# S5 powers and chunk angles between the first projections, small copies on VectorE, and a head's split in two steps

## The chip, the cores and the metric

One core of one Trainium2 chip runs the whole kernel: TensorE (PE), VectorE (DVE), ScalarE (ACT) and GpSimd (POOL) beside SyncE (SP), which only issues transfers. The metric is device microseconds of one execution of the kernel, the median of several runs.

## What is computed

A backbone of two layers over 1024 latent tokens and 256 context tokens of 1024 channels. The even layer, in which the change lies, projects the normed tokens and runs two recurrences over the sequence in both directions: a real one (RG-LRU, 8 heads of 128 channels, behind a centred convolution of 4 taps) and a complex diagonal one (S5, 32 groups of 16 channels and 64 states). The odd layer is latent attention, and is not touched.

```python
def even_mix(h_ctx, h_lat, ...):
    xa_l, ga_l, ub_l, gb_l = jnp.split(h_lat @ w_in, EVEN_SPLITS, axis=-1)   # the same for ctx
    ya_c, ya_l = rglru_mix(xa_c, xa_l, conv_w, conv_b, wr, br, wi, bi, lam, with_ctx)
    yb_c, yb_l = s5_mix(ub_c, ub_l, lam_re, lam_im, log_dt, b_re, b_im, c_re, c_im, d_skip, glu_w, glu_b, with_ctx)
    return concat([ya * silu(ga), yb * silu(gb)]) @ w_out

def rglru_coeffs(u, wr, br, wi, bi, lam):          # u: convolved input of the head
    r = sigmoid(u @ wr + br); i = sigmoid(u @ wi + bi)
    log_a = -LRU_C * r * softplus(-lam)
    return exp(log_a), sqrt(-expm1(2 * log_a)) * (i * u)   # then h[t] = a h[t-1] + b

def s5_discretise(lam_re, lam_im, log_dt, b_re, b_im):
    dt = exp(log_dt); mag = exp(lam_re * dt)
    ab_re = mag * cos(lam_im * dt); ab_im = mag * sin(lam_im * dt)
    f = (ab - 1) / lam                             # complex
    return ab, f * b                               # then h[t] = ab h[t-1] + (f b) u[t]
```

## The kernel before, in words

All of it is one program for one core, written out in the order in which each engine gets its instructions; no scheduler reorders them. Matrix products take fp32 operands as a high part (`hi`, a cast on ScalarE) and a low part (`lo`, the difference, on VectorE) and add three products (`mm3`, L209 to L211). Tokens stand as 128 channels by 1280 columns (NT: 256 context, 1024 latent).

`start` (from L531, its last part is touched) norms the tokens and runs the first projections in pairs of 128 output channels, kept in PSUM banks `mm` and `g`. `pair` is a generator: each `next(run)` issues a part of a pair's products on PE, and between two of them the code puts work for the other engines. In order around the change: the pair with weights `w2` (heads 0 and 1 of the RG-LRU input); `convolve(h, banks)` for each of the two heads, that is `conv_in` (two ScalarE passes out of each bank into `xa` and `u`), three `conv_tap` on VectorE and `conv_parts`, which makes `hi` and `lo` of `u`; the pair with weights `w3` (S5 inputs); `lru_prep` (26 tiny VectorE operations on `lrusp`); `s5_small`, which makes 19 powers of each S5 eigenvalue (`Pre`, `Pim`), calls `s5_phases` and then makes the input factors `bb`. At step 7 of that last pair the first weights of the recurrence stage are split (`wh` L751, `wl` L752), and the S5 inputs leave PSUM as `chunks` (L603).

`s5_phases` (L431) makes, for 16 batches of two groups, the angle of every chunk of 8 tokens: four pieces, each of three VectorE operations (L438 to L440), four ScalarE activations (L441 to L444) and three transfers of 640 KB into the DRAM buffer `phdr`, issued by POOL (L446). The tiles of `big` (line 150) are 11 buffers of 5 KB a partition that are shared round-robin; a tile waits until the one that had its buffer before is done with, transfers included. `setup` is a pool of its own, opened in the space of an earlier pool once that is released.

`recurrences` runs 8 turns, one for each head. The order of each turn is written out by hand in `TURNS` (L64): the first row for turns 0 and 1, the second for turns 2 to 6, the third for turn 7. A word is a step, its arguments, and by how many turns its head or batch is older than the turn (`-`: one ahead). Capitals are steps of a head: `C` a tap, `I` the split `hi`, `lo`, `G` gate products, `A H Q` exponent, tanh and root on ScalarE, `M B D N` products and scan on VectorE. Small letters are steps of an S5 batch (three in each of turns 2 to 6, one in turn 7; L63): `l` loads, `k` decay, `a` products on PE, `s` rotation into `G` (L966 to L969), `r` the two scans over chunks into `H` (L977 to L982), `d` rotation back (L987 to L990), `o` products on PE and ScalarE's copy `y` (L1000). `P` are projection products and `W` weights that fill PE between.

Two of these steps end in a small copy on ScalarE: `s` extends G by its first 32 columns, `r` moves 32 columns of H behind two POOL memsets:

```python
tt(S, S, x.t2, ALU.add)
nc.scalar.copy(x.G[:, :, :, NCH:EXT], x.G[:, :, :, 0:32])     # L969, end of s
...
nc.gpsimd.memset(Hv[64:128, :, :, EXT - 1:EXT], 0.0)
nc.scalar.copy(Hv[64:128, :, :, 0:32], Hv[64:128, :, :, NCH:EXT])   # L982, end of r
```

Of the kernel before, what the change touches and what calls it, by code (L numbers as in the profile page):

```python
# [19 lines left out]
CH, NCH = 8, 160  # L20
# [12 lines left out]
def shape_constants():  # L33
# [18 lines left out]
    for a in (row, col):  # L52
# [80 lines left out]
class Kernel:  # L133
# [225 lines left out]
    def s5_small(self):  # L359
        nc, t, c, sp = self.nc, self.t, self.const, self.sp  # L360
        tt, ts, stt = nc.vector.tensor_tensor, nc.vector.tensor_scalar, nc.vector.scalar_tensor_tensor
        LR, LI, LD = self.s5p[:, 0], self.s5p[:, 1], self.s5p[:, 2]
        sm = sp.tile([128, 12, 32], F32, name="s5small")
        dt, lr, th, n_, u, den, nr, fr, fi, x1, x2 = (sm[:, i] for i in range(11))
        self.s5_rho = c.tile([128, 32], F32, name="s5rho")
        self.s5_u8 = c.tile([128, 32], F32, name="s5u8")
        nc.scalar.activation(dt, LD, AF.Exp)
        tt(lr, LR, dt, ALU.mult)
# [7 lines left out]
        NP = 19  # L376
        v = sp.tile([128, 32, NP], F32, name="s5v", tag="vx", bufs=4)
        w = sp.tile([128, 32, NP], F32, name="s5w", tag="vx", bufs=4)
        bc = lambda a, k: a.unsqueeze(2).to_broadcast([128, 32, k])
        kpow = sp.tile([128, 2, NP], F32, name="s5k")  # L380
        nc.sync.dma_start(kpow, t["kpow"])
        kk = lambda i: kpow[:, i].unsqueeze(1).to_broadcast([128, 32, NP])
        tt(v, bc(u, NP), kk(0), ALU.mult)
        ts(w, v, MAGIC, -MAGIC, ALU.add, ALU.add)
        tt(v, v, w, ALU.subtract)
# [7 lines left out]
        tt(w, bc(lr, NP), kk(1), ALU.mult)
        nc.scalar.activation(w, w, AF.Exp)
        nc.vector.tensor_copy(self.s5_rho, w[:, :, 18])
        Pre, Pim = hs, sn
        tt(Pre, hs, w, ALU.mult)
        tt(Pim, sn, w, ALU.mult)
        self.s5_phases()
# [31 lines left out]
    def s5_phases(self):  # L431
# [3 lines left out]
        for q in range(4):  # L435
# [4 lines left out]
            nc.vector.tensor_sub(v, v, n)  # L440
            nc.scalar.activation(n, v, AF.Abs)  # L441
# [89 lines left out]
    def start(self, outs):  # L531
# [91 lines left out]
        with self.tc.manual_schedule():  # L623
# [10 lines left out]
            self.load_const("s5p", "tau", "lru", "dmask", "s5d")  # L634
# [76 lines left out]
            for i in range(8):  # L711
# [144 lines left out]
    def recurrences(self, steps):  # L856
# [8 lines left out]
        class Head:  # L865
# [59 lines left out]
            def I(x):  # L925
                self.conv_parts(x.h)

        class Batch:
# [31 lines left out]
            def s(x):  # L960
# [8 lines left out]
                nc.scalar.copy(x.G[:, :, :, NCH:EXT], x.G[:, :, :, 0:32])  # L969

            def r(x):
# [10 lines left out]
                nc.scalar.copy(Hv[64:128, :, :, 0:32], Hv[64:128, :, :, NCH:EXT])  # L982
# [135 lines left out]
        def run(w, n):  # L1118
# [7 lines left out]
            elif (2 if k in "CI" else 0) <= n - age < 8:  # L1126
# [665 lines left out]
```

## Time and profile before

| what | value |
|---|---|
| median of 3 runs | 1636.22 us (1633.61 to 1636.89) |
| the profiled execution, its own time | 1638.18 us |
| its span (first to last instruction) | 1636.3 us |
| PE busy | 1504.2 us (92%) |
| VectorE, ScalarE, POOL busy | 1140.8, 835.5, 39.2 us |
| mean granted TensorE clock | 0.962 of full |

The profile is of one execution. The page gives busy time of each engine and the groups of costliest instructions; the trace behind it gives each instruction with its start, its duration and, in brackets, how long the engine idled before it and which instruction or transfer ended that (`<-`). The busy time includes nothing of register and semaphore instructions. Names on the left of `<-` in an instruction are what it writes, on the right what it reads; L is the line of the kernel.

### The profile page before, as it was taken

How to read it: one execution, taken by the hardware profiler on the slowest of the kernel's cores; microseconds unless marked ns; L12 is line 12 of the kernel's file. 1: busy time of each engine (PE TensorE's matmuls, PEld its weight loads, DVE VectorE, ACT ScalarE, POOL GpSimd, SP SyncE). 2: the span in 40 equal slices, each digit the busy share in tenths (PEclk: the TensorE clock that was granted, in tenths of full speed). 3: DMA queues.
4: the chain of work that ended last, by engine and by line, in shares of the span. 5: the costliest groups of instructions: out<-in, count | busy, mean ns of one | idle time of the engine just before them, and what ended most of it. 6: DMA issues, size and time to landing. Idle time of an engine off the chain costs nothing.

```text
span 1636.3 us, 22534 instructions
## 1 busy us (share of the span) xinstructions
PE 1504.2 (92%) x8690; PEld 1293.7 (79%) x8690; DVE 1140.8 (70%) x1827; ACT 835.5 (51%) x1441; POOL 39.2 (2%) x98
## 2 busy tenths in 40 slices
PE   7893797988888988799999999999999999999997
PEld 4672686776777777687787899978999999999887
DVE  6865479888988978832226443557888888889755
ACT  6544566586668567311115321545556555556532
POOL 0001100000000000000000000010000000000000
PEclk9897799999999999799999999999999999999999
DMA  9342542543435345555543132244011020122253
GB/s 352 104 143 97 199 140 88 175 125 117 133 106 163 118 136 200 214 206 180 190 150 139 52 104 78 81 163 134 17 46 55 30 70 19 56 91 84 78 179 124
DMA packets 94698, 201.93 MB, mean 123 GB/s; under 512 B 9728, under 2 KB 42240, under 8 KB 94592
## 3 DMA queue, kind: packets, MB, share of 16 engines
q1 hardware_dynamic: 86240, 166.03, 30.6%
q0 software_dynamic: 8352, 34.48, 5.6%
q8 instruction: 68, 1.11, 0.3%
q14 instruction: 38, 0.31, 0.1%
HBM read 142.41 MB, written 58.06 MB: 123 GB/s over the span
## 4 chain that ended last, share of the span: by engine, by line
PE 38%; issue 27%; DVE 16%; ACT 9%; DMA 3%; POOL 1%; SPq 0%; DVEq 0%; POOLq 0%; ACTq 0%
PE pv L1537 7%; PE pt L1524 4%; PE S L209 2%; PE S L211 2%; PE S L210 2%; PE mm L211 2%; PE S L1474 2%; PE S L1476 2%; PE S L1475 2%; PE S L1473 2%; PE mm L209 2%; PE S L1472 2%; PE mm L210 2%; DVE H L977 2%; DVE H L978 1%
## 5 line engine op out<-in xcount | busy, mean ns | idle before, releaser
L182 ACT CAST w_hi<-wraw 128x1024 fp32r<-128x1024 f32 (+3 forms) x73 | 63.0, 864 | 196.6 <-PE mm L210 130.8
L209 PE MATMUL mm<-n0hi,w_hi 128*128 128x512 f32 (+1 forms) x432 | 157.5, 365 | 0.0
L211 PE MATMUL mm<-n0hi,w_lo 128*128 128x512 f32 (+1 forms) x432 | 155.1, 359 | 0.0
L210 PE MATMUL mm<-n0lo,w_hi 128*128 128x512 f32 (+1 forms) x432 | 154.9, 359 | 0.0
L1528 ACT CAST ph<-pt 128x512 fp32r<-128x512 f32 x160 | 90.9, 589 | 83.2 <-PE pt L1524 82.5
L1531 DVE TENSOR_TENSOR pl<-pt,ph 128x512 fp32r<-128x512 f32 x160 | 109.5, 686 | 19.5 <-ACT ph L1528 17.6
L209 PE MATMUL mm<-hi,w_hi 128*128 128x512 f32 (+1 forms) x264 | 101.3, 384 | 12.1 <-ACT w_hi L182 9.9
L209 PE MATMUL mm<-n1hi,w_hi 128*128 128x342 f32 (+2 forms) x336 | 109.5, 329 | 1.6 <-DVE pr L1280 1.6
L210 PE MATMUL mm<-n1lo,w_hi 128*128 128x342 f32 (+2 forms) x336 | 110.7, 330 | 0.0
L211 PE MATMUL mm<-n1hi,w_lo 128*128 128x342 f32 (+2 forms) x336 | 110.3, 328 | 0.0
L1537 PE MATMUL pv<-ph,v 128*128 128x256 f32 x640 | 107.3, 298 | 0.0
L184 DVE TENSOR_TENSOR w_lo<-wraw,w_hi 128x1024 fp32r<-128x1024 f32 (+3 forms) x73 | 72.4, 991 | 45.6 <-ACT w_hi L182 43.9
L211 PE MATMUL mm<-hi,w_lo 128*128 128x512 f32 (+1 forms) x264 | 99.6, 380 | 4.6 <-DVE w_lo L184 4.6
L210 PE MATMUL mm<-lo,w_hi 128*128 128x512 f32 (+1 forms) x264 | 99.8, 378 | 0.2 <-DVE lo L1155 0.2
L209 PEld LDWEIGHTS mm<-n0hi,w_hi 128*128 128x128 f32 x432 | 82.7, 191 | 12.7
L210 PEld LDWEIGHTS mm<-n0lo,w_hi 128*128 128x128 f32 x432 | 82.6, 191 | 12.8
L211 PEld LDWEIGHTS mm<-n0hi,w_lo 128*128 128x128 f32 x432 | 82.2, 190 | 12.6
L1524 PE MATMUL pt<-c_ident,P 128*128 128x128 f32 x640 | 90.9, 272 | 0.6 <-DVE kl L1454 0.6
L1509 ACT ACTIVATE P<-S,sm 128x512 f32<-128x512 f32 x128 | 86.6, 688 | 0.0
L1537 PEld LDWEIGHTS pv<-ph,v 128*128 128x128 f32 x640 | 84.2, 190 | 0.2
L1524 PEld LDWEIGHTS pt<-c_ident,P 128*128 128x128 f32 x640 | 75.6, 140 | 10.3 <-DVE kl L1454 0.9
L1501 DVE TENSOR_REDUCE sm<-S 128x1 f32<-128x512 f32 x128 | 82.1, 681 | 0.7 <-PE S L1476 0.7
(421 smaller groups left out, 4046.9 us busy)
## 6 DMA issues: line engine op xcount, KB each, us to landing
mw<-in_mod_w SPq DMA_DIRECT2D x48, 512.0 KB
wraw<-in_w_in SPq DMA_DIRECT2D x24, 512.0 KB
s5wt<-s5scr SPq DMA_DIRECT2D x16, 512.0 KB
ph<-phdr SPq DMA_DIRECT2D x16, 480.0 KB
wraw<-in_mla_in SPq DMA_DIRECT2D x14, 512.0 KB
wraw<-in_w_out SPq DMA_DIRECT2D x16, 384.0 KB
xT<-in_xT SPq DMA_DIRECT2D x8, 640.0 KB
ga<-gadr SPq DMA_DIRECT2D x8, 640.0 KB
```

What stands on the lines that cost most here:

```text
L182: nc.scalar.copy(hi, raw)
L184: nc.vector.tensor_sub(lo, raw, hi.bitcast(F32))
L209: mm(out, w[0], x[0], start=start, stop=False)
L210: mm(out, w[0], x[1], start=False, stop=False)
L211: mm(out, w[1], x[0], start=False, stop=stop)
L977: scan(H[up, 2:2 + n], fl(x.rho, up), fl(x.G, up), 0.0, ALU.mult, ALU.add)
L1501: nc.vector.reduce_max(x.sm[e][:, n:n + 1], x.S[e][n], axis=mybir.AxisListType.X)
L1509: nc.scalar.activation(x.P[e][:, s:s + z], x.S[e][n], AF.Exp, bias=sm[:, 4:5], scale=SCALE, accum_out=sm[:, 5 + n:6 + n])
L1524: nc.tensor.transpose(pt[:, i, e], x.P[e][:, key:key + 128], self.ident)
L1528: nc.scalar.copy(x.hi[t], x.pt[t])
L1531: nc.vector.tensor_sub(x.lo[t], x.pt[t], x.hi[t].bitcast(F32))
L1537: mm(x.pv, v[:, 128 * (h % 2):128 * (h % 2) + 128], p, start=x.left == 30, stop=x.left == 1)
```

## The change

The S5 powers move to `s5_turns`, with tiles from `big`, called at step 6 of the pair of heads 0 and 1; `kpow`, its table of exponents, becomes a constant loaded at the start. `s5_phases` becomes a generator that yields behind each piece's VectorE part and behind its ScalarE part and transfers; the pieces are drawn between `conv_in`, the taps and parts of the two heads, the last ScalarE part after the pair with `w3`. `s5_small` copies the powers into the `setup` pool and goes on from there, at step 1 of that pair; `lru_prep` follows at step 2. Raw weights 20 are loaded where `w3`'s second part is split. In the recurrences both small copies go from ScalarE to VectorE, and `I` becomes `I` (the cast) and `O` (the difference), at places of their own in the first two rows of `TURNS`. No product on PE changes its place.

```diff
@@ TURNS
-     "W0 Y1 E0 A10 E0 Q00 E0 P0 E0 E0 E0 E0 E0 E0 C1- C2- P0 E0 I-").split(),
+     "W0 Y1 E0 A10 E0 Q00 E0 P0 E0 E0 E0 E0 E0 E0 C1- C2- I- P0 E0 O-").split(),
...
-     "k00 s00 P0 r00 d00 C1- W0 Y1 P0 G110 o00 k10 G010 a10 C0- s10 M00 V0- V1- A10 r10 A00 H00 Q00 C2- "
-     "d10 I- P0 l20 P0 B00 o10").split(),
+     "k00 s00 P0 r00 d00 C1- W0 Y1 P0 G110 o00 k10 G010 a10 C0- s10 M00 V0- V1- C2- A10 r10 A00 H00 I- Q00 "
+     "d10 P0 O- l20 P0 B00 o10").split(),
@@ s5_small -> s5_turns, s5_small
+    def s5_turns(self):
+        sm = self.big([128, 5, 32], name="s5a")
...
+        v, w, sn, hs = (self.big([128, 32, NP], name=n) for n in ("s5v", "s5w", "s5sin", "s5half"))
...
+        tt(hs, hs, w, ALU.mult)
+        tt(sn, sn, w, ALU.mult)
+        return hs, sn
+
+    def s5_small(self, hs, sn):
...
+        Pre, Pim = (sp.tile([128, 32, 19], F32, name=n) for n in ("s5pre", "s5pim"))
+        nc.vector.tensor_copy(Pre, hs)
+        nc.vector.tensor_copy(Pim, sn)
...
-        self.s5_phases()
@@ s5_phases
             nc.vector.tensor_sub(v, v, n)
+            yield
             nc.scalar.activation(n, v, AF.Abs)
...
                                   a.rearrange("p (b g) c -> p b (g c)", b=4))
+            yield
@@ start
-            self.load_const("s5p", "tau", "lru", "dmask", "s5d")
+            self.load_const("s5p", "kpow", "tau", "lru", "dmask", "s5d")
...
-                    if i == 5:
-                        r = raw(19)
+                    r = raw(19 if i == 5 else 20)
+                if i == 6:
+                    powers = self.s5_turns()
+            phases = self.s5_phases()
+            next(phases)
             self.xa, self.us = {}, {}
-            self.convolve(0, ps[0])
+            for b, p in enumerate(ps[0]):
+                self.conv_in(0, p, b)
+            for _ in range(2):
+                next(phases)
             mp.release()
             self.gp = self.pool("gw")
             self.sp = self.pool("setup")
             next(run)
-            next(run)
-            self.convolve(1, ps[1])
+            ps = next(run)
+            for b, p in enumerate(ps[1]):
+                self.conv_in(1, p, b)
+            for h in range(2):
+                for i in range(3):
+                    self.conv_tap(h, i)
+                self.conv_parts(h)
+                for _ in range(2):
+                    next(phases)
             run = pair(w3, self.n0)
-            self.lru_prep()
-            small = self.s5_small()
+            small = None
             for i in range(10):
                 ps = next(run)
-                if i == 0:
-                    r = raw(20)
+                if i == 1:
+                    small = self.s5_small(*powers)
+                if i == 2:
+                    self.lru_prep()
...
+            for _ in phases:
+                pass
@@ recurrences, Head
             def I(x):
-                self.conv_parts(x.h)
+                del self.xa[x.h]
+                x.hi = self.big([128, NT], F32R, name="hi")
+                nc.scalar.copy(x.hi, self.us[x.h][0])
+
+            def O(x):
+                lo = self.big([128, NT], F32R, name="lo")
+                nc.vector.tensor_sub(lo, self.us[x.h][0], x.hi.bitcast(F32))
+                self.us[x.h] += x.hi, lo
@@ recurrences, Batch: s, r
-                nc.scalar.copy(x.G[:, :, :, NCH:EXT], x.G[:, :, :, 0:32])
+                nc.vector.tensor_copy(x.G[:, :, :, NCH:EXT], x.G[:, :, :, 0:32])
...
-                nc.scalar.copy(Hv[64:128, :, :, 0:32], Hv[64:128, :, :, NCH:EXT])
+                nc.vector.tensor_copy(Hv[64:128, :, :, 0:32], Hv[64:128, :, :, NCH:EXT])
```

VectorE's queue in `start`, before: the end of the second angle piece, the third and the fourth (`phase` and `cosine` are a piece's tiles, in brackets the counters that a row waits for; `DMASW` are the transfers that POOL issues).

```order
L440 TENSOR_TENSOR phase_981<-phase_981,cosine_982 128x1280 [waits DVE_49]
L438 TENSOR_TENSOR phase_994<-s5u_938,c_tau 128x1280 [waits DMASW3_49,Activation_49]
L439 TENSOR_SCALAR cosine_995<-phase_994 128x1280 [waits DMASW4_49,DVE_49]
L440 TENSOR_TENSOR phase_994<-phase_994,cosine_995 128x1280 [waits DVE_49]
L438 TENSOR_TENSOR phase_1007<-s5u_938,c_tau 128x1280 [waits DMASW6_49,Activation_49]
L439 TENSOR_SCALAR cosine_1008<-phase_1007 128x1280 [waits DMASW7_49,DMASW2_49,DVE_49]
L440 TENSOR_TENSOR phase_1007<-phase_1007,cosine_1008 128x1280 [waits DVE_49]
L401 TENSOR_SCALAR s5small<-s5half 128x32
```

The pieces stood one behind another, and `s5small` behind them. Now, from the end of the second piece to the copies of the powers (`u` rows are taps of heads 0 and 1, `lo` their low parts):

```order
L446 TENSOR_TENSOR phase_902<-phase_902,cosine_903 128x1280 [waits DVE_49]
L864 SCALAR_TENSOR_TENSOR u_888<-xa_887,c_lru,u_888 128x254 [waits DMASW1_49,Activation_49]
...
L1186 TENSOR_TENSOR lo_949<-u_888,hi_947 128x1280 [waits Activation_49]
L444 TENSOR_TENSOR phase_958<-s5u_822,c_tau 128x1280 [waits DMASW4_49]
L445 TENSOR_SCALAR cosine_959<-phase_958 128x1280 [waits DMASW5_49,DVE_49,Activation_49]
L446 TENSOR_TENSOR phase_958<-phase_958,cosine_959 128x1280 [waits DVE_49]
L864 SCALAR_TENSOR_TENSOR u_934<-xa_933,c_lru,u_934 128x254
...
L1186 TENSOR_TENSOR lo_972<-u_934,hi_970 128x1280 [waits DMASW7_49,DMASW3_49,Activation_49]
L444 TENSOR_TENSOR phase_981<-s5u_822,c_tau 128x1280 [waits DMASW0_49,Activation_49]
L445 TENSOR_SCALAR cosine_982<-phase_981 128x1280 [waits DMASW1_49,DVE_49]
L446 TENSOR_TENSOR phase_981<-phase_981,cosine_982 128x1280 [waits DVE_49]
L404 COPY s5pre<-s5half_826 128x608 [waits DMAHW6_49]
```

The third piece stands ahead of head 1's taps and waits for POOL's transfers of the first piece (`DMASW4`, its negative sines) and of the second (`DMASW5`, its cosines); the fourth waits for two transfers of the third (POOL's transfers take the eight counters in turn, so that `DMASW0` is here the third piece's cosines and `DMASW1` its phases).

ScalarE's queue in turn 4 of the recurrences, before, from the G copy (`a` is the exponent of a head's gate, `r` tanh and root, `gw_hi` gate weights):

```order
L969 COPY G_3497<-G_3497 128x4x32
L182 CAST gw_hi_3505<-gwraw_3292 128x256
L182 CAST gw_hi_3509<-gwraw_3195 128x256
L890 ACT_TABLE_LOAD
L890 ACTIVATE a_3513<-r_3261,lrus 128x1280
L982 COPY H_3515<-H_3515 64x4x32
L890 ACTIVATE a_3521<-r_3204,lrus 128x1280
L894 ACTIVATE r_3204<-r_3204,lrus 128x1280
L897 ACT_TABLE_LOAD
L897 ACTIVATE r_3204<-r_3204 128x1280
L1153 CAST hi_3530<-u_3258 128x1280
L1052 ACT_TABLE_LOAD
```

Now, from the same gate weights:

```order
L182 CAST gw_hi_3510<-gwraw_3297 128x256
L182 CAST gw_hi_3514<-gwraw_3200 128x256
L914 ACT_TABLE_LOAD
L914 ACTIVATE a_3520<-r_3266,lrus 128x1280
L914 ACTIVATE a_3528<-r_3209,lrus 128x1280
L918 ACTIVATE r_3209<-r_3209,lrus 128x1280
L952 CAST hi_3531<-u_3263 128x1280
L921 ACT_TABLE_LOAD
L921 ACTIVATE r_3209<-r_3209 128x1280
L1083 ACT_TABLE_LOAD
```

The two copies are gone, and the cast `hi` stands ahead of the table load and the root. On VectorE the same stretch of the turn now reads:

```order
L1000 COPY G_3502<-G_3502 128x4x32
L924 TENSOR_TENSOR i_3477<-i_3477,u_2841 128x1280
...
L864 SCALAR_TENSOR_TENSOR u_3263<-xa_3262,c_lru,u_3263 128x255
L864 SCALAR_TENSOR_TENSOR u_3263<-xa_3262,c_lru,u_3263 128x1023
L1008 SCALAR_TENSOR_TENSOR H_3522<-rho_3474,G_3502 64x768
L1009 SCALAR_TENSOR_TENSOR H_3522<-rho_3474,G_3502 64x768
L1013 COPY H_3522<-H_3522 64x4x32
L1018 TENSOR_TENSOR t_563_3501<-ph_3351,H_3522 128x640
L1020 TENSOR_TENSOR G_3502<-H_3522,ph_3351 128x4x160
L1021 TENSOR_TENSOR G_3502<-G_3502,t_563_3501 128x4x160
L956 TENSOR_TENSOR lo_3566<-u_3263,hi_3531 128x1280
```

Both copies stand here, the first behind the sum of `G`, the second between the scans and `t`; the tap (L864) moved ahead of the scans, and `lo` is the last row as before.

## Rows read from the trace of the kernel before

**Rows 1.** The page: busy time by engine, and bytes moved.
```profile
PE 1504.2 (92%) x8690; PEld 1293.7 (79%) x8690; DVE 1140.8 (70%) x1827; ACT 835.5 (51%) x1441; POOL 39.2 (2%) x98
...
DMA packets 94698, 201.93 MB, mean 123 GB/s; under 512 B 9728, under 2 KB 42240, under 8 KB 94592
```

**Rows 2.** Windows: length, busy us per engine (instructions), PE clock, DMA share, GB/s.
```profile
140.00:160.00 20.00, 0.00 (x0) 0.00 (x0) 7.96 (x7) 13.63 (x11) 4.50 (x6) 0.55 0.44 159
...
452.74:507.88 55.14, 48.10 (x241) 41.07 (x240) 49.69 (x53) 37.46 (x55) 1.12 (x7) 0.94 0.40 129
```

**Rows 3.** PE's timeline after the hole: start, duration, instruction, [idle <-releaser].
```profile
172.08 0.58 PE L209 MATMUL mm<-n0hi,wh 128*128 128x256 f32 x1 [34.97 <-ACT chunks L603]
...
173.08 0.58 PE L211 MATMUL mm<-n0hi,wl 128*128 128x256 f32 x1 [0.20 <-DVE wl L752]
```

**Rows 4.** VectorE's timeline from the S5 powers to the first recurrence weights.
```profile
100.15 0.69 DVE L279 COPY row<-s 128x512 f32<-128x512 f32 x1 [4.12 <-PE s L277]
...
105.87 4.85 DVE L840 SCALAR_TENSOR_TENSOR u<-xa,c_lru,u 128x254 f32<-128x254 f32 x6
...
122.41 0.17 DVE L807 TENSOR_SCALAR lrusp<-lrusp 128x16 f32<-128x16 f32 x1
...
127.11 0.18 DVE L368 TENSOR_TENSOR s5small<-c_s5p,s5small 128x32 f32<-128x32 f32 x1
...
136.55 1.48 DVE L438 TENSOR_TENSOR phase<-s5u,c_tau 128x1280 f32<-128x1280 f32 x1
...
140.34 1.48 DVE L438 TENSOR_TENSOR phase<-s5u,c_tau 128x1280 f32<-128x1280 f32 x1
...
152.82 1.49 DVE L438 TENSOR_TENSOR phase<-s5u,c_tau 128x1280 f32<-128x1280 f32 x1 [8.61 <-DMA phdr<-phase]
...
154.55 0.83 DVE L439 TENSOR_SCALAR cosine<-phase 128x1280 f32<-128x1280 f32 x1 [0.23 <-DMA phdr<-negsin]
...
165.08 0.35 DVE L401 TENSOR_SCALAR s5small<-s5half 128x32 f32<-128x32 f32 x1
...
167.45 0.65 DVE L426 TENSOR_TENSOR vx<-s5small,vx 128x512 f32<-128x512 f32 x1
...
171.80 1.22 DVE L752 TENSOR_TENSOR wl<-wraw,wh 128x1024 fp32r<-128x1024 f32 x1 [0.30 <-ACT wh L751]
```

**Rows 5.** ScalarE's timeline: input copies of head 1, sines of two pieces.
```profile
111.98 0.36 ACT L832 COPY xa<-g 128x256 f32<-128x256 f32 x1
...
114.31 0.82 ACT L833 ACTIVATE u<-g,c_lru 128x512 f32<-128x512 f32 x1
...
140.46 1.27 ACT L441 ACTIVATE cosine<-phase 128x1280 f32<-128x1280 f32 x1 [5.45 <-DVE phase L440]
...
145.51 1.34 ACT L444 ACTIVATE cosine<-cosine,half_pi 128x1280 f32<-128x1280 f32 x1
...
151.00 1.27 ACT L442 ACTIVATE negsin<-phase 128x1280 f32<-128x1280 f32 x1 [2.98 <-DMA phdr<-cosine]
```

**Rows 6.** VectorE's waits, 200 to 640 us: us in total, times, longest.
```profile
DVE lo L1155 <- ACT hi L1153: 16.0, 6, 3.0
...
DVE H L977 <- ACT G L969: 5.6, 10, 1.3
DVE t L987 <- ACT H L982: 5.4, 9, 1.2
```

**Rows 7.** Timelines of ACT, DVE and POOL in one turn of the recurrences.
```profile
456.46 0.30 ACT L982 COPY H<-H 64x128 f32<-64x128 f32 x1 [2.02 <-POOL H L981]
...
462.04 1.24 ACT L1153 CAST hi<-u 128x1280 fp32r<-128x1280 f32 x1
...
463.31 1.49 DVE L1155 TENSOR_TENSOR lo<-u,hi 128x1280 fp32r<-128x1280 f32 x1 [3.00 <-ACT hi L1153]
...
456.32 0.10 POOL L981 MEMSET H<- 64x4 f32 x1 [1.63 <-DVE H L978]
```

**Rows 8.** VectorE's timeline: a small copy.
```profile
191.24 0.28 DVE L469 COPY pad<-s5bb 64x256 f32<-64x256 f32 x1
```

More of the change, by code (lines that the diff above doesn't have):

```diff
@@ L356, in spread @@
         return banks
-    def s5_small(self):
-        nc, t, c, sp = self.nc, self.t, self.const, self.sp
+    def s5_turns(self):
+        nc, c = self.nc, self.const
         tt, ts, stt = nc.vector.tensor_tensor, nc.vector.tensor_scalar, nc.vector.scalar_tensor_tensor
-        LR, LI, LD = self.s5p[:, 0], self.s5p[:, 1], self.s5p[:, 2]
-        sm = sp.tile([128, 12, 32], F32, name="s5small")
-        dt, lr, th, n_, u, den, nr, fr, fi, x1, x2 = (sm[:, i] for i in range(11))
+        LI, LD = self.s5p[:, 1], self.s5p[:, 2]
+        sm = self.big([128, 5, 32], name="s5a")
+        dt, lr, th, n_, u = (sm[:, i] for i in range(5))
         self.s5_rho = c.tile([128, 32], F32, name="s5rho")
         self.s5_u8 = c.tile([128, 32], F32, name="s5u8")
+        NP = 19
+        v, w, sn, hs = (self.big([128, 32, NP], name=n) for n in ("s5v", "s5w", "s5sin", "s5half"))
+        bc = lambda a: a.unsqueeze(2).to_broadcast([128, 32, NP])
+        kk = lambda i: self.kpow[:, i].unsqueeze(1).to_broadcast([128, 32, NP])
         nc.scalar.activation(dt, LD, AF.Exp)
-        tt(lr, LR, dt, ALU.mult)
+        tt(lr, self.s5p[:, 0], dt, ALU.mult)
+        tt(w, bc(lr), kk(1), ALU.mult)
+        nc.scalar.activation(w, w, AF.Exp)
         tt(th, LI, dt, ALU.mult)
@@ L375, in s5_small @@
         ts(u, u, INV_2PI, None, ALU.mult)
[L376 to L385, printed above, removed]
+        tt(v, bc(u), kk(0), ALU.mult)
+        ts(sn, v, MAGIC, -MAGIC, ALU.add, ALU.add)
+        tt(v, v, sn, ALU.subtract)
         nc.vector.tensor_copy(self.s5_u8, v[:, :, 18])
-        sn = sp.tile([128, 32, NP], F32, name="s5sin")
-        hs = sp.tile([128, 32, NP], F32, name="s5half")
+        nc.vector.tensor_copy(self.s5_rho, w[:, :, 18])
+        nc.scalar.activation(hs, v, AF.Sin, scale=ONE_PI)
         nc.scalar.activation(sn, v, AF.Sin, scale=TWO_PI)
-        nc.scalar.activation(hs, v, AF.Sin, scale=ONE_PI)
         tt(hs, hs, hs, ALU.mult)
         ts(hs, hs, -2.0, 1.0, ALU.mult, ALU.add)
[L393 to L398, printed above, removed]
-        self.s5_phases()
+        tt(hs, hs, w, ALU.mult)
+        tt(sn, sn, w, ALU.mult)
+        return hs, sn
+    def s5_small(self, hs, sn):
+        nc, t, sp = self.nc, self.t, self.sp
+        tt, ts = nc.vector.tensor_tensor, nc.vector.tensor_scalar
+        LR, LI = self.s5p[:, 0], self.s5p[:, 1]
+        sm = sp.tile([128, 7, 32], F32, name="s5small")
+        den, nr, fr, fi, x1, x2, _ = (sm[:, i] for i in range(7))
+        bc = lambda a, k: a.unsqueeze(2).to_broadcast([128, 32, k])
+        Pre, Pim = (sp.tile([128, 32, 19], F32, name=n) for n in ("s5pre", "s5pim"))
+        nc.vector.tensor_copy(Pre, hs)
+        nc.vector.tensor_copy(Pim, sn)
         ts(nr, Pre[:, :, 17], -1.0, None, ALU.add)
@@ L1125, in run @@
                     getattr(bs[a[0]], k)()
-            elif (2 if k in "CI" else 0) <= n - age < 8:
+            elif (2 if k in "CIO" else 0) <= n - age < 8:
                 getattr(heads[n - age], k)(*a)
```

## The prediction

> **What bounds the kernel now.** I read the page first: TensorE (PE) is busy for 92% of the span [rows 1], so time is won only where PE stands still or where something else sets the pace. The busy time by stretch shows the two places that the change touches. Between 140 and 160 us PE does nothing at all, and from about 200 to 640 us, where the recurrences run, one turn of the loop takes 55.14 us with PE busy for 48.10, VectorE (DVE) for 49.69 and ScalarE (ACT) for 37.46 [rows 2].
>
> The hole: PE's own timeline names it, 34.97 us of idling that end with ACT's chunk copies, and one matmul later PE waits for `wl`, VectorE's low part of the next weights [rows 3]. What VectorE does until then is a chain, read from its timeline [rows 4] beside ScalarE's [rows 5]: `lrusp` (122.41 to 127.11), the S5 powers (to 136.55), four chunk-angle pieces, the small S5 factors (165.08 to 167.45), the input factors `s5bb` (to 171.50), `wl` (to 173.02). The third and fourth pieces stand still for transfers to `phdr`, since their buffers are those of earlier pieces: piece 3 waits 8.61 us. The hole is as long as this chain, not as PE's work.
>
> The turn: VectorE's 49.69 us leave 5.45, and the table of waits names what it waits for over all turns: `lo` for ACT's `hi` 16.0 us, the scan for the G copy 5.6 us, the product `t` for the H copy 5.4 us, 27.0 together [rows 6]. Nothing comparable is named, so VectorE sets this stage. The instructions of one turn show why ACT is late [rows 7]: it waits in order for the H copy's sources (2.02 us), then does a, a, r, a table load and the root, and only then casts `hi` at 462.04; VectorE, ready since about 460.3, starts `lo` at 463.31 after 3.00 us.
>
> **Startup, step by step.** The change takes nothing off: it starts the chain earlier, and adds two copies of 608 columns. VectorE is free at 100.84, when the `row` copy ends. I lay the new order out with the old durations (VectorE, ACT, transfers from the same rows, all [rows 4, 5]).
> - The powers took 9.44 us (127.11 to 136.55), with both table loads inside: they end at 110.3. `w_lo` of the next weights (1.22 plus a gap) to 111.7; the first piece 3.79 and the small `gw_lo` parts, to 116.0. ACT's sines of piece 1 are four activations of 1.27 to 1.34, ends overlapping, about 5.05: 116.0 to 121.05.
> - ACT's second input copies (the six of a head took 111.98 to 115.13, 3.15) end at 124.2, VectorE's taps of head 0 (4.85) at 124.6, the cast `hi` at 126.45, sines of piece 2 at 131.45.
> - Piece 3 stands behind that on VectorE: its second product needs the transfer of piece 2's cosine. Here cosines landed 4.15 us after ACT's last activation of the piece (146.85 to 151.00), phases 5.97 (152.82), negative sines 7.70 (154.55). So that product starts at 135.6 and the piece ends at 137.95 (0.83 and 1.49). **This is the new wait**, and behind it stand the taps of head 1 (to 142.8), their `hi` (144.1), and the sines of piece 3 (149.1).
> - Piece 4's second product needs piece 3's phase: 149.1 + 5.97 = 155.1, and the piece ends at 157.45. Then on VectorE: the two copies, priced at 0.45 each (a scaling of 1280 columns took 0.83, by width 0.39 for 608; the copy of 256 took 0.28 [rows 8], by width 0.67; I take a value near the first, whose size is nearer), 158.3; small factors 2.37; `s5bb` 4.05; `lrusp` 4.70, which now stands behind them; `wl` 1.22: 170.7. Before it was 173.02.
>
> The gain is **2.3 us**. PE gets no nearer because the chain is still one of transfers: the two landings took the place of the two old waits. The arrays of a piece land 1.8 us apart, so if each of the two landings is one array earlier or later, this is 2.3 ± 3.6: between 5.9 gained and 1.3 lost. Of what I cost at nothing: the last sines lie behind the chunk copies on ACT, with no reader before the recurrences; the load of `kpow` (128 rows of 38 numbers, 19 KB) moves to the start, into SP's queue ahead of `tau`; at the page's mean of 123 GB/s [rows 1] it is 0.16 us, its upper end, and PE waits there for the large loads issued before it.
>
> **Recurrences, step by step.** All three edits act on the 27.0 us. The cast `hi` now comes after a, a, r, ahead of the table load and root: 2.5 us earlier, and 2.02 earlier again because ACT no longer waits for the H sources, while VectorE comes to `lo` later by its own copies. So the 16.0 of `lo` should go, and the 11.0 of the two copy waits go with the copies. What it costs is VectorE's time, on the engine that sets the pace: two copies of 128 columns for each of 16 batches. ACT's took 0.30 [rows 7]; VectorE's of 256 columns on 64 partitions 0.28 [rows 8]. I take 0.25 for each, nearer to the latter with half its width, and 0.20 for the H copy's wait on POOL's memset (scan end 456.26 to the ACT copy at 456.46 [rows 7]), which now has nothing of VectorE's to hide behind: 0.70 a batch, 11.2 in all. Bounds: 0.3 a batch (half of 0.28 twice, the hop hidden) is 4.8; 1.0 (0.28 twice, the hop twice) is 16. Net **27.0 - 11.2 = 15.8 us** (11 to 22); a turn with three batches goes from 55.14 to about 52.2, still above PE's 48.10. Late next is PE's order: 7.0 us of waits a turn, which shrink only as VectorE's results come earlier.
>
> **Sum.** The profiled execution took 1638.18: 1638.18 - 2.3 - 15.8 = 1620.1. It lies 1.96 above the median of the runs, 1636.22, so the median should be **1618**, between 1608 and 1628 with both bounds.
>
> **Rivals.**
> A. *The turn does not follow VectorE.* PE is busy 48.10 and waits 7.0 for its operands; if those waits hang on ACT's evacuations and not on VectorE, the turn stays near 55.1, and only the startup is left: 1636.2 - 2.3 = 1634. For it: PE is as tightly packed as VectorE within 1.6 us. Against it: VectorE's waits are listed and all three kinds are touched. Chance 0.08, anything between 1628 and 1639 counted with it.
> B. *Slower: VectorE is full, and the copies only add.* If `lo` goes on waiting, because ACT's `hi` stands behind the sigmoids and the tanh instead, and the copies' waits turn into VectorE's own waits for PE's products, then 11.2 us are added in full: 1636.2 - 2.3 + 11.2 = 1645. This decides if the waits that go are worth less than the copies cost; the break-even is 27.0/16 = 1.69 us a batch, against 0.70 that I take. For it: VectorE is busy 49.69 of 55.14 [rows 2]. Against it: the upper bound is 1.0. Chance 0.05. The Trainium skill (Perfetto Trace Analysis, section Optimizing Scalar/DVE Operations) speaks against this edit: it advises to move work to ScalarE where VectorE is saturated, and the change does the opposite. By that rule the turn gets longer and the kernel ends near 1645. The trace bears out that VectorE is the fuller engine, but also that each copy on ACT makes it stand still for longer than the copy lasts [rows 6, 7].
> C. *The hole closes to PE's own work.* If the transfers land well before they are waited for, VectorE's chain has slack of its own: PE's products of this stage would end near 146 (137.1 before, plus the 9 us by which ACT frees the `g` banks later, 121.05 against 111.98 [rows 5], since sines now stand ahead of the second copies), and PE would start again near 148, not 170.7: 22 us more, 1596. Against it: 8.61 us of waiting for such a transfer in the trace [rows 4], with no more buffers than before. Chance 0.07.
>
> **Numbers.** My forecast has 0.80, A 0.08, B 0.05, C 0.07. Range: the forecast's own bounds, reached up to A's 1634 and down by 2 for a part of C: 1606 to 1634. A measurement of this kernel can tell about 0.2%, 3.3 us, from no change. Faster takes the forecast and C, 0.87; the same is A, 0.08; slower B, 0.05.
>
> **What would show it.** In the changed kernel's profile: PE starting again at about 170.7, released by `wl`; VectorE's `cosine` product of piece 3 waiting some 10 us for `phdr<-cosine`, and that of piece 4 for `phdr<-phase`; turns of 52.2 us; no wait of `lo` for `hi`; VectorE's H copy waiting 0.2 for POOL. The prediction is wrong if PE's hole ends before 165 or after 174 (the walk), if the turns stay above 54 (A, B), or if VectorE's copies take over 0.5 (the price).

## The result, and the profile after

The changed kernel takes 1611.24 us (median of 4 runs, 1611.05 to 1611.67), the kernel before 1635.31 (4 runs, 1633.61 to 1636.89): a ratio of 0.985, 95% interval [0.9838, 0.9863]. That is 24.1 us less, where 18.2 were forecast; the time lies inside the range. The profiled execution has a span of 1609.5 us against 1636.3, 26.8 less, since that of the kernel before lay above its median.

The line of the page that answers to [rows 1]: VectorE does 6 us more work than before, ScalarE 9 less, and PE's same matmuls take 10 us less.

```profile
PE 1494.5 (93%) x8690; PEld 1285.7 (80%) x8690; DVE 1147.2 (71%) x1861; ACT 826.3 (51%) x1409; POOL 39.4 (2%) x98
```

**The startup.** PE's timeline of the changed kernel, the first matmuls behind a longer idle time (it answers to [rows 3]):

```profile
121.51 0.58 PE L209 MATMUL g<-n0hi,w_hi 128*128 128x256 f32 x1 [4.46 <-ACT u L857]
...
159.68 0.58 PE L209 MATMUL mm<-n0hi,wh 128*128 128x256 f32 x1 [12.41 <-ACT chunks L611]
...
170.07 0.58 PE L211 MATMUL mm<-n0hi,wl 128*128 128x256 f32 x1 [9.59 <-DVE wl L774]
```

PE waits 4.46 us for the second head's input copies, which ScalarE now does behind the sines of the first piece. The hole is broken in two (12.41 and 9.59 us) by one pair of matmuls that need only `wh`, and ends with `wl` at 170.07, where it was 173.08. It is shorter than the 34.97 of [rows 3] mainly because PE's products ahead of it end later (at 147.27 us, before at 137.11); what counts is the 3.0 us at its end. VectorE's timeline of the same stretch (it answers to [rows 4]):

```profile
109.45 0.78 DVE L393 TENSOR_TENSOR s5sin<-s5sin,s5w 128x608 f32<-128x608 f32 x1
...
128.65 1.49 DVE L444 TENSOR_TENSOR phase<-s5u,c_tau 128x1280 f32<-128x1280 f32 x1 [0.99 <-DMA phdr<-negsin]
...
135.20 0.83 DVE L445 TENSOR_SCALAR cosine<-phase 128x1280 f32<-128x1280 f32 x1 [5.05 <-DMA phdr<-cosine]
...
152.70 1.49 DVE L444 TENSOR_TENSOR phase<-s5u,c_tau 128x1280 f32<-128x1280 f32 x1 [7.51 <-DMA phdr<-cosine]
...
154.74 0.83 DVE L445 TENSOR_SCALAR cosine<-phase 128x1280 f32<-128x1280 f32 x1 [0.55 <-DMA phdr<-phase]
...
157.00 0.47 DVE L404 COPY s5pre<-s5half 128x608 f32<-128x608 f32 x1
...
168.80 1.22 DVE L774 TENSOR_TENSOR wl<-wraw,wh 128x1024 fp32r<-128x1024 f32 x1
```

The powers end at 110.23 (forecast 110.3). The third piece's second product waits 5.05 us for piece 2's cosine to land and starts at 135.20 (forecast 135.6). Of the fourth piece it is the first product that waits long, 7.51 us for piece 3's cosine; its second product then waits 0.55 for piece 3's phase and starts at 154.74 (155.1); a copy of the powers takes 0.47 (0.45); `wl` ends at 170.02 (170.7).

**The turn.** Window of one turn of the recurrences, from the second batch's scan to the same scan one turn on (columns as in [rows 2]):

```profile
440.72:492.94 52.22, 46.36 (x241) 39.71 (x240) 50.86 (x59) 35.90 (x48) 1.13 (x7) 0.97 0.43 134
```

52.22 us instead of 55.14, as forecast (52.2), and VectorE is busy for 50.86 of them. VectorE's timeline in that turn, with the two copies, and ScalarE's cast (they answer to [rows 7]):

```profile
436.91 0.23 DVE L1000 COPY G<-G 128x128 f32<-128x128 f32 x1
...
437.06 1.49 DVE L924 TENSOR_TENSOR i<-i,u 128x1280 f32<-128x1280 f32 x1
...
444.44 0.23 DVE L1013 COPY H<-H 64x128 f32<-64x128 f32 x1 [0.19 <-POOL H L1012]
...
447.04 1.48 DVE L956 TENSOR_TENSOR lo<-u,hi 128x1280 fp32r<-128x1280 f32 x1
```

```profile
440.83 1.27 ACT L952 CAST hi<-u 128x1280 fp32r<-128x1280 f32 x1 [1.46 <-DVE u L864]
```

The G copy has a duration of 0.23, and the next instruction starts 0.15 after the copy's start. The H copy waits 0.19 for POOL and the instruction behind it starts 0.26 after its start, 0.45 together. So a batch costs 0.60 where 0.70 were taken. `lo` at 447.04 has no idle time ahead of it: `hi` was done at 442.10, 4.9 us before.

**Where the rest came from.** The waits of VectorE in the recurrences of the changed kernel (us in total, times, longest), and under them a wait of the kernel before from the same table as [rows 6]:

```profile
DVE w_lo L184 <- ACT w_hi L182: 4.8, 1, 4.8
DVE H L1013 <- POOL H L1012: 3.1, 16, 0.2
```

```profile
DVE w_lo L184 <- ACT w_hi L182: 9.1, 2, 5.0
```

`w_lo` for the weights' cast was 9.1 us in the table of before and is 4.8 now. In the kernel before, one of its two waits comes from the H copy too. ScalarE's and VectorE's timelines of turn 7 of the kernel before:

```profile
589.51 0.30 ACT L982 COPY H<-H 64x128 f32<-64x128 f32 x1 [6.16 <-POOL H L981]
...
592.30 1.03 ACT L182 CAST w_hi<-wraw 128x1024 fp32r<-128x1024 f32 x1
```

```profile
593.36 1.23 DVE L184 TENSOR_TENSOR w_lo<-wraw,w_hi 128x1024 fp32r<-128x1024 f32 x1 [4.04 <-ACT w_hi L182]
```

ScalarE stood 6.16 us, in order, for the H copy's source, and the root and the weights' cast stood behind it; VectorE waited 4.04 us for them. Turn 7, measured from the scan of the fourth batch from the end to that of the last (three batches on, as in a steady turn), fell from 69.26 us (546.38 to 615.64) to 62.05 (527.08 to 589.13): 7.2 us, which is 4.3 more than a steady turn's 2.9.

Part of the rest is PE's clock. Windows of 5 us at the start of turn 2, over about the same matmuls, of the kernel before, of the changed one, and of experiment 1 below, which has the new startup and the old recurrences:

```profile
308.00:313.00 5.00, 5.00 (x22) 4.52 (x21) 5.00 (x4) 4.04 (x5) 0.00 (x0) 0.53 0.74 222
```

```profile
303.00:308.00 5.00, 5.00 (x37) 4.65 (x36) 5.00 (x4) 4.77 (x8) 0.00 (x0) 1.00 0.53 164
```

```profile
304.00:309.00 5.00, 5.00 (x37) 4.65 (x36) 5.00 (x4) 4.92 (x8) 0.00 (x0) 1.00 0.69 195
```

PE is busy throughout in all three, but at a granted 0.53 (near the lower level) for 22 matmuls before, at 1.00 for 37 in the other two. The whole stretch from `wl` to the first scan over chunks took 152.0 us before (173.08 to 325.06) and 147.8 after (170.07 to 317.88). In experiment 1 it took 148.9 (170.02 to 318.88), though PE waited there just ahead of these matmuls as it did in the kernel before: 1.5 us for `hi` and 1.1 for `lo`. So 3.1 of the 4.2 us were there without the edits of the recurrences, with the clock; the other 1.1 is about the 0.9 us of the one early `lo`.

### The profile page after: what moved, and what is told of

Its sections match the earlier page's. It is cut to its first block, busy times and chain, and to the rows that moved or that the text cites. A ratio compares the mean times of both kernels' runs of the same rounds, so it can differ in the third digit from the quotient of the medians.

```text
span 1609.5 us, 22558 instructions
## 1 busy us (share of the span) xinstructions
PE 1494.5 (93%) x8690; PEld 1285.7 (80%) x8690; DVE 1147.2 (71%) x1861; ACT 826.3 (51%) x1409; POOL 39.4 (2%) x98
## 4 chain that ended last, share of the span: by engine, by line
PE 35%; issue 23%; DVE 3%; DMA 2%; ACT 1%; POOL 1%; SPq 0%; DVEq 0%; POOLq 0%; ACTq 0%
PE pv L1568 7%; PE pt L1555 4%; PE S L209 2%; PE S L211 2%; PE S L210 2%; PE S L1507 2%; PE S L1506 2%; PE S L1505 2%; PE S L1503 2%; PE S L1504 2%; PE mm L209 1%; PE mm L211 1%; PE mm L210 1%; PE pt L210 1%; PE pt L211 1%
```

## The experiments

Each kernel was timed in three rounds beside the kernel before, whose median was 1635.51 us beside the first four, 1636.29 beside the next four, 1635.49 beside the last three. Diffs are against the changed kernel unless said otherwise.

**1. The startup alone.** The changed kernel without its edits of the recurrences:

```diff
-                nc.vector.tensor_copy(x.G[:, :, :, NCH:EXT], x.G[:, :, :, 0:32])
+                nc.scalar.copy(x.G[:, :, :, NCH:EXT], x.G[:, :, :, 0:32])
...
-                nc.vector.tensor_copy(Hv[64:128, :, :, 0:32], Hv[64:128, :, :, NCH:EXT])
+                nc.scalar.copy(Hv[64:128, :, :, 0:32], Hv[64:128, :, :, NCH:EXT])
...
-     TURNS rows 1 and 2 with I- and O-
+     TURNS rows 1 and 2 as before, I calls conv_parts, no O
```

> The changed kernel with both edits of the recurrences undone (small copies back on ScalarE, split in one step at its old place); the startup stays as changed. My theory: startup and recurrences add up; PE starts again for good at about 170 us instead of 173.08, and nothing else moves: 1635.3 - 3.0 = 1632 us. Rival (the startup also changes the clock or the loads of the turns behind it, and so carries part of the 9 us that the steady turns don't explain): 1623 to 1629.

Measured: 1632.09 us, ratio 0.9981 [0.9971, 0.9990]. PE's timeline has the hole of the changed kernel:

```profile
159.49 0.58 PE L209 MATMUL mm<-n0hi,wh 128*128 128x256 f32 x1 [11.98 <-ACT chunks L611]
...
170.02 0.58 PE L211 MATMUL mm<-n0hi,wl 128*128 128x256 f32 x1 [9.73 <-DVE wl L774]
```

The expectation held: the startup is worth 3.4 us, about what `wl` comes earlier, and the rest lies in the recurrences. The first scan over chunks was 6.2 us earlier than in the kernel before (318.88 against 325.06), the last only 4.7 us earlier (610.94 against 615.64): the 3.1 us by which the clock shortened the stretch ahead of the first scan were in part lost again to the pace of the turns. Only one execution of each kernel is traced, so whether the others had that clock too is not shown.

**2. The recurrences alone.** The kernel before with both edits of the recurrences (copies, `I` and `O`).

> The kernel before with only the edits of the recurrences. My theory: steady turns of 52.2 us (before 55.15), 15 us in five turns, and some 6 us more in turns 1 and 7, where PE's clock no longer falls: 1635.3 - 21 = 1614 us, and the steady turns the same length as in the changed kernel. Rival (part of the gain needs the new startup): 1618 to 1624.

Measured: 1613.96 us, ratio 0.9870 [0.9855, 0.9885], turns of 52.23. As expected, the two parts add up: 3.4 + 21.5 = 24.9, measured together 24.1. Against the expectation PE's granted clock still falls at the start of turn 2 here, though for a shorter time (0.76 and 0.56 in two windows of 2.5 us, 1.00 behind them).

**3. The copies back on ScalarE**, the split still in two steps:

```diff
-                nc.vector.tensor_copy(x.G[:, :, :, NCH:EXT], x.G[:, :, :, 0:32])
+                nc.scalar.copy(x.G[:, :, :, NCH:EXT], x.G[:, :, :, 0:32])
...
-                nc.vector.tensor_copy(Hv[64:128, :, :, 0:32], Hv[64:128, :, :, NCH:EXT])
+                nc.scalar.copy(Hv[64:128, :, :, 0:32], Hv[64:128, :, :, NCH:EXT])
```

> The changed kernel with both small copies back on ScalarE, the cast and the difference still apart. My theory: the copies on VectorE cost 0.60 a batch and remove 0.70 of waits, so they are worth little by themselves, but ScalarE again waits for their sources ahead of the cast: turns of 52.3 to 53.2 us, 1612 to 1617 us. Rival (VectorE is full, and the copies on it are pure cost, the rule against this edit): turns of 50.4 us, 1602 us. Second rival (the copies carry most of the gain): turns above 54, above 1620 us.

Measured: 1638.29 us, ratio 1.0018 [1.0006, 1.0031]; turns of 56.7 to 57.2. My theory fell here, and the second rival was right: the copies carry the gain, and the split without them costs 6.2 us against experiment 1. ScalarE's timeline of a turn, and VectorE's `lo`:

```profile
454.15 0.30 ACT L1013 COPY H<-H 64x128 f32<-64x128 f32 x1 [3.34 <-POOL H L1012]
...
457.14 1.24 ACT L952 CAST hi<-u 128x1280 fp32r<-128x1280 f32 x1
```

```profile
458.41 1.49 DVE L956 TENSOR_TENSOR lo<-u,hi 128x1280 fp32r<-128x1280 f32 x1 [1.51 <-ACT hi L952]
```

The tap now stands ahead of the scans, so ScalarE comes to the H copy earlier relative to its source, and waits 3.34 us where it waited 2.02 [rows 7]. The cast did move ahead of the root, and `lo` waits 1.51 instead of 3.00; but the turn got longer all the same, since VectorE waits longer for both copies (G 16.6 us in all, H 8.0, against 5.6 and 5.4 in [rows 6]).

**4. The split joined again**, the copies on VectorE: `TURNS` and `I` as before, no `O`.

> The changed kernel with the split in one step at its old places, the copies on VectorE. My theory: the cast stands behind table load and root again, but ScalarE no longer waits for the H copy's sources ahead of it, so VectorE's lo waits about 1 us a turn instead of 3: turns of 53 us, and the loss of the clock at the first turns comes back: 1616 to 1621 us. Rival (the split alone carries the 3.0 us a turn): turns of 55 us, 1626 us or more. Second rival (the copies alone did it): turns of 52.2, 1611 us.

Measured: 1611.60 us (1611.11 to 1612.72), ratio 0.9853 [0.9837, 0.9870], turns of 52.16. The second rival was right: the copies alone did it. VectorE's waits, 200 to 600 us, and ScalarE's cast in a steady turn:

```profile
DVE H L1006 <- POOL H L1005: 3.1, 16, 0.2
...
DVE lo L1179 <- ACT hi L1177: 0.9, 1, 0.9
```

```profile
440.82 1.27 ACT L921 ACTIVATE r<-r 128x1280 f32<-128x1280 f32 x1
444.96 1.26 ACT L1177 CAST hi<-u 128x1280 fp32r<-128x1280 f32 x1 [2.87 <-DVE u L864]
```

Of `lo`'s 16.0 us [rows 6] one wait of 0.9 is left, ahead of the first steady turn. The cast stands behind table load and root as in the kernel before, and yet it is in time, because ScalarE no longer stands still for two copies ahead of it: it is through with the root at 442.09 and waits 2.87 us for the tap that the cast reads. `lo` starts at 447.18, 1.0 us behind the cast's end.

**5 and 6. One copy at a time**, from experiment 4: only G on VectorE, then only H.

```diff
-                nc.vector.tensor_copy(Hv[64:128, :, :, 0:32], Hv[64:128, :, :, NCH:EXT])
+                nc.scalar.copy(Hv[64:128, :, :, 0:32], Hv[64:128, :, :, NCH:EXT])
```

> As the last run of the group before (new startup, split in one step at its old place), with only the G copy on VectorE and the H copy on ScalarE. New theory: the gain of the recurrences is ScalarE's standing still, in order, ahead of the cast and of the weight casts; the H copy's wait for POOL (36 us in the kernel before) and the G copy's wait for VectorE (28 us) both do that. Of the 20.5 us between both copies on ScalarE (1632.1) and both on VectorE (1611.6) the G copy alone is then worth about 28/65, 9 us: 1623 us, turns near 54. Rival (only the H copy counts, since it stands between scan and cast): 1631 us, turns of 55. Rival (only the G copy counts): 1612.

Measured: 1631.83 us, ratio 0.9976 [0.9967, 0.9986], turns of 54.96: nothing against 1632.09. The theory of shares fell; the first rival was right here. VectorE's waits (200 to 600 us), and ScalarE's (180 to 640):

```profile
DVE lo L1179 <- ACT hi L1177: 16.0, 6, 3.0
...
DVE t L1011 <- ACT H L1006: 5.5, 9, 1.3
```

```profile
ACT H L1006 <- POOL H L1005: 53.1, 14, 6.6
```

Freed of the wait for G, ScalarE comes to the H copy earlier and waits there instead: 53.1 us, where the table of before had 36.2 for H and 28.4 for G. `hi` is as late as before.

```diff
-                nc.vector.tensor_copy(x.G[:, :, :, NCH:EXT], x.G[:, :, :, 0:32])
+                nc.scalar.copy(x.G[:, :, :, NCH:EXT], x.G[:, :, :, 0:32])
```

> The mirror of it: the H copy on VectorE, the G copy on ScalarE. New theory: 36/65 of 20.5 us, about 11: 1621 us, turns near 53.5; VectorE's lo still waits for the cast about 1 us. Rival (only H counts): 1612 us. Rival (only G counts): 1631 us. If the sum of both single gains is less than 20.5, the two waits cover each other and have to go together.

Measured: 1614.25 us, ratio 0.9874 [0.9858, 0.9890], turns of 52.53, and turn 7 down to 62.03 us from 70.01 in experiment 1. The rows that answer, of VectorE (200 to 600 us) and of ScalarE (180 to 640):

```profile
DVE H L1001 <- ACT G L993: 6.4, 10, 1.3
...
DVE lo L1179 <- ACT hi L1177: 0.9, 1, 0.9
```

```profile
ACT G L993 <- DVE G L992: 34.3, 10, 5.0
```

ScalarE's cast and VectorE's `lo` in a steady turn:

```profile
450.86 1.24 ACT L1177 CAST hi<-u 128x1280 fp32r<-128x1280 f32 x1
```

```profile
452.14 1.49 DVE L1179 TENSOR_TENSOR lo<-u,hi 128x1280 fp32r<-128x1280 f32 x1
```

The H copy is worth 17.8 us (1632.09 to 1614.25), the G copy with it 2.7 more (to 1611.60). ScalarE stands 34.3 us for G, about as long as it stood for H, and the cast is still in time, if only just: it ends at 452.10 and `lo` starts at 452.14 without a wait. Of the two in-order waits nearly everything hung on the last one before the cast. How much of the 2.7 is G's is open: the turns give 0.37 each, but the traced execution was also the longest of its four (1618.03 us), with PE's clock at the lower level at the start of turn 2 (0.66 and 0.50 in two windows of 2.5 us) and its first scan at 322.41, where experiment 4 had 1.00 and 318.12.

**7. The H copy twice:**

```diff
+                nc.vector.tensor_copy(Hv[64:128, :, :, 0:32], Hv[64:128, :, :, NCH:EXT])
```

> The changed kernel with the H copy on VectorE written twice in a row (16 instructions more, the same result). If VectorE now sets the turn, three more of 0.15 to 0.26 us lengthen it from 52.21 to 52.7 to 53.0, and the time by 2.4 to 4.2 us: 1614 to 1615.5. Rival (PE or ScalarE sets the turn now): no change, 1611.2.

Measured: 1617.82 us (1616.80 to 1619.25), turns of 52.99, that is 0.78 a turn for three copies of 0.26. VectorE's timeline:

```profile
445.03 0.23 DVE L1013 COPY H<-H 64x128 f32<-64x128 f32 x1 [0.19 <-POOL H L1012]
...
445.29 0.23 DVE L1014 COPY H<-H 64x128 f32<-64x128 f32 x1
...
445.55 0.82 DVE L1019 TENSOR_TENSOR t<-ph,H 128x640 f32<-128x640 f32 x1
```

VectorE sets the turn now, to the last 0.26 us. The time lies above the expected 1614 to 1615.5, all the same. In the profiled executions the last scan came 2.6 us later than in the changed kernel (591.72 against 589.13), and some 3.8 us more were lost behind it, in stages that the edit does not touch; what did that stays open.

**8. The rest of the startup chain behind `wl`:**

```diff
-                for _ in range(2):
+                for _ in range(2 - h):
                     next(phases)
...
-                if i == 1:
-                    small = self.s5_small(*powers)
-                if i == 2:
-                    self.lru_prep()
...
+                if i == 8:
+                    small = self.s5_small(*powers)
+                    self.lru_prep()
```

> The changed kernel with the rest of the startup chain behind the first weights of the recurrences: the fourth angle piece, the copies of the powers, the small factors and lrusp come after wl on VectorE. My theory: PE stood still for 12.4 and 9.6 us only for VectorE's order; wl then ends near 151 instead of 170, and VectorE has 17.8 us of idle time behind it for what was moved: 1611.2 less 15 to 19 us, 1592 to 1596 us. Rival (the S5 steps of the first turn need these factors, so the hole only moves behind them): 1606 to 1612 us.

Measured: 1598.19 us (1596.21 to 1601.19), ratio 0.9772 [0.9756, 0.9789]. PE's timeline, and VectorE's:

```profile
152.36 0.39 PE L209 MATMUL mm<-n0hi,wh 128*128 128x256 f32 x1 [4.01 <-ACT chunks L611]
...
175.23 0.58 PE L209 MATMUL g<-hi,gw_hi 128*128 128x256 f32 x1 [5.36 <-ACT i L908]
```

```profile
150.04 1.23 DVE L770 TENSOR_TENSOR wl<-wraw,wh 128x1024 fp32r<-128x1024 f32 x1 [4.33 <-ACT wh L769]
...
173.42 1.22 DVE L184 TENSOR_TENSOR w_lo<-wraw,w_hi 128x1024 fp32r<-128x1024 f32 x1 [6.32 <-ACT w_hi L182]
```

The hole shrinks to 4.01 us, and PE is through with `wl`'s first use 17.3 us earlier; the time falls by 13.0. Some 3 us are given back at once, where PE waits 5.36 us for the gates: ScalarE's sines of the fourth piece now stand ahead of them (`w_lo` waits 6.32 for the cast behind the sines; the changed kernel's longest wait of PE for gates is 1.7 there). PE's granted clock fell here at the start of turn 2 as well, to a mean of 0.74 between 290 and 295 us; what that took of the remaining 1.3 us is not shown.

**9. The H copy on POOL**, from experiment 4:

```diff
-                nc.vector.tensor_copy(Hv[64:128, :, :, 0:32], Hv[64:128, :, :, NCH:EXT])
+                nc.gpsimd.tensor_copy(Hv[64:128, :, :, 0:32], Hv[64:128, :, :, NCH:EXT])
```

> New startup, split in one step at its old place, G copy on VectorE, and the H copy on POOL, right behind the memset that it waited for. If ScalarE's standing in order before the H copy was the loss, it is gone here as well, and only VectorE's own wait for a copy on another engine is left (16 copies, each longer than on VectorE by a hop and POOL's slower work, 0.3 to 0.8 us): 1611.6 + 5 to 13 = 1616 to 1624 us, and lo no longer waits 3 us a turn. Rival (VectorE's direct wait for the H copy was the loss): nothing is gained against the copy on ScalarE, 1630 us or more.

Measured: 1613.92 us, ratio 0.9869 [0.9855, 0.9884], turns of 51.95, a little shorter than with the copy on VectorE. POOL's timeline, and VectorE's wait:

```profile
465.62 0.10 POOL L1005 MEMSET H<- 64x4 f32 x1 [1.62 <-DVE H L1002]
...
465.79 0.29 POOL L1006 COPY H<-H 64x128 f32<-64x128 f32 x1
```

```profile
DVE t L1011 <- POOL H L1006: 5.3, 11, 0.6
```

VectorE waits for the copy 11 times, 5.3 us in all, as it did for ScalarE's (9 times, 5.4 us [rows 6]); and still 18 of the 20.5 us are there, more than expected. So it was not VectorE's wait for the copy that cost the time, but that ScalarE stood for its source. The turn is 0.2 us shorter than in experiment 4 and the time 2.3 longer: here PE ran at the lower clock level at the start of turn 2, and the first scan came at 321.12 instead of 318.12, though the two kernels issue the same work up to there.

**10. Only `lrusp` behind `wl`:**

```diff
-                if i == 2:
-                    self.lru_prep()
...
+                if i == 8:
+                    self.lru_prep()
```

> The changed kernel with lrusp alone behind wl. If the hole of PE is as long as VectorE's chain up to wl, wl comes 4.7 us earlier, at about 164 of the span, and of that what the run before showed for the rest (13 us of time for 17.3 us of hole) should reach the end: 1611.2 - 3.5 to 4.7 = 1606.5 to 1608 us. Rival (ScalarE's exponent for lrusp, with its table load, stands ahead of the gates then): 1611 us.

Measured: 1608.80 us, but from 1604.27 to 1611.01; ratio 0.9830 [0.9807, 0.9853], which overlaps the changed kernel's [0.9838, 0.9863]. PE's timeline:

```profile
157.82 0.58 PE L209 MATMUL mm<-n0hi,wh 128*128 128x256 f32 x1 [9.62 <-ACT chunks L611]
...
166.12 0.58 PE L211 MATMUL mm<-n0hi,wl 128*128 128x256 f32 x1 [7.50 <-DVE wl L772]
```

The hole ends 3.95 us earlier; how much of it reaches the end these runs don't tell.

**11. Experiment 8, refined:** the two copies of the powers ahead of `wl`, the fourth piece first behind it.

```diff
+                if i == 1:
+                    Pre, Pim = (self.sp.tile([128, 32, 19], F32, name=n) for n in ("s5pre", "s5pim"))
+                    nc.vector.tensor_copy(Pre, powers[0])
+                    nc.vector.tensor_copy(Pim, powers[1])
...
+                if i == 9:
+                    next(phases)
+                    small = self.s5_small(Pre, Pim)
+                    self.lru_prep()
```

> The version with the rest of the startup behind wl, refined: the two copies of the powers ahead of wl, where VectorE idled 4.3 us for the cast of wh (so that the chunk copy on ScalarE no longer waits for them), then the fourth angle piece, then the small factors and lrusp. PE starts about 1 us earlier, and ScalarE's sines of the fourth piece come some 6 us earlier, ahead of the gates that PE waited 5.4 us for: 1598.2 - 3 to 6 = 1592 to 1595 us. Rival (the tables that ScalarE loads between sines and Silu give it back): 1597 to 1599 us.

Measured: 1597.66 us (1593.67 to 1598.94), ratio 0.9764 [0.9747, 0.9781]: not to be told from experiment 8. PE starts 3.0 us earlier than there,

```profile
149.36 0.39 PE L209 MATMUL mm<-n0hi,wh 128*128 128x256 f32 x1 [2.94 <-ACT chunks L608]
...
150.35 0.58 PE L211 MATMUL mm<-n0hi,wl 128*128 128x256 f32 x1 [0.49 <-DVE wl L771]
```

and the last scan over chunks comes 3.0 us earlier (572.47 against 575.50), but the spans of the profiled executions are equal (1596.2 and 1596.3): it is lost in the stages behind the recurrences, and the runs don't show to what. Both versions are faster than the changed kernel by 13 us and than the kernel before by 38.

## Why the prediction was right, and where not

*The startup* held term by term. The walk that laid the new order out with the old durations came within 0.7 us at `wl`, and found the two landings that hold VectorE up. Worth 2.3 by forecast, 3.0 in the trace, 3.4 alone. Of its signs two came out otherwise: the third piece's product waited 5.05 us for the cosine and not some 10, and of the fourth piece the long wait (7.51) stood one product earlier, for the cosine and not for the phase.

*The turn* held in size (52.2), but not in its cause. The step that failed is "All three edits act on the 27.0 us. The cast `hi` now comes after a, a, r, ahead of the table load and root". The 16.0 us of `lo` were put down to the cast's place. Experiment 4 takes that place back and loses nothing that could be measured; experiment 3 keeps it and loses everything. What made `hi` late was the H copy ahead of it. Its wait (2.02 us) and the copy itself (0.30) leave ScalarE, and VectorE comes to `lo` 0.45 later by its own copy: 2.77 of the 3.00, and in experiment 6, with the H copy alone moved, the wait of `lo` is gone in every steady turn. The sum named the 2.02 as a second help beside the cast's 2.5. With the G copy off ScalarE too, the cast waits for the tap whichever way cast and root are ordered (1.46 us in the changed kernel, 2.87 in experiment 4). That the size of the turn came out was luck in this: the edit to which the sum's largest term was put down gives nothing here, and the one counted beside it gives the whole.

*The size outside the steady turns* was missed: 5.9 us of the median. Against a sum for the profiled execution of 18.1 stand 26.8 in the spans. The startup gave 0.7 more; turn 7 gave 4.3 more than a steady turn; and the stretch from `wl` to the first scan got 4.2 shorter, where the sum had the 0.9 of one early `lo`: 3.3 more. That is 8.3 of the 8.7. "Nothing comparable is named" was wrong: the same table had `w_lo` for `w_hi` with 9.1 us, of which 4.04 hung on the H copy, and at its head a wait of turns 0 and 1:

```profile
DVE s5K L521 <- ACT s5K L520: 16.4, 6, 5.6
```

The 3.3 go with the clock at the start of turn 2, which PE had at the lower level before and not after. Six kernels with the same two waits of PE ahead of it (1.5 and 1.1 us) bear that out: from `wl` to the first scan three took 148.2 to 148.9 us with the clock at 1.00 (experiments 1, 4 and 5), three 151.4 to 152.0 with the lower one (the kernel before, experiments 6 and 9). The edits of the recurrences don't decide which, since experiment 1 lacks them and experiments 6 and 9 have some; so some 3 of the 26.8 us between the two spans are not shown to be the change's work. The copies were cheaper than taken (0.60 a batch, not 0.70), without the turn getting shorter than forecast. And the forecast's own bounds give 1626.5 at the upper end (11.0 us gained and 1.3 lost), not 1628; nothing hung on that.

*Rival A* (the turn stays at 55.1): no, PE's busy time in a turn fell with the rest, 48.10 to 46.36, at a mean clock of 0.97 instead of 0.94. *Rival B* (copies only add on a full VectorE): each copy does add its 0.26 us to the turn, as experiment 7 shows, but the break-even of 1.69 us a batch was far off at 0.60. The Trainium skill, which the prediction set behind this rival (Perfetto Trace Analysis, section Optimizing Scalar/DVE Operations), says no more than that offloading some work to ScalarE may make sense where VectorE is saturated. This case goes the other way: with VectorE busy for 90% of the turn, moving two copies onto it took 20.5 us off. *Rival C* (the hole closes): not in the changed kernel. The landings held VectorE up until 154.74 as argued, but from there to 170.02 it worked on what stood ahead of `wl` in its queue; experiment 8 moves that and the fourth piece behind `wl`, closes the hole to 4.01 us, and gives 1598 where C had 1596.

One sentence ahead of the prediction is too strong: where two stages meet, the framework does interleave their instructions, as the `gw_lo` of the recurrences between the rows of an angle piece show. It bore on no term.

## What to carry to other kernels

In an engine that works in order, look not at how long a small instruction takes but at how long the engine stands ahead of it, and what stands behind: three copies of 0.30 us on ScalarE cost a turn 2.6 us (experiment 6 against 1). Put a short dependent step on the engine that makes its source, even if that engine is the fullest one, or on one that has nothing queued behind it. And where PE waits for one result, move ahead of everything else on that engine what makes it: that gave another 13 us here.

## What the runs showed of the hardware

The same copy of 64 partitions by 128 columns took 0.23 us on VectorE, 0.30 on ScalarE and 0.29 on POOL (where one of the sixteen took 1.46); on POOL the turn was shortest (51.95 us, 52.16 with the copy on VectorE), and that this is because nothing waits behind it there is argued, not shown. Two kernels with the same work up to the first scan (experiments 4 and 9) came to it at 318.12 and 321.12 us: in one of them PE's granted clock was at the lower level for the matmuls behind its short waits for `hi` and `lo`, in the other not. Ahead of both it waited for the same 1.5 and 1.1 us. What decides that is open; at about 3 us it is as large as some of the effects measured here.
